# A hybrid decoder layer: all mixers ahead of the feed-forward, and gate and up projections of two token blocks as seven products of halves

## The chip, the core and the metric

The kernel runs on one core of a Trainium2 chip. A core has five engines that work side by side, each with its own queue of instructions in a fixed order: TensorE (PE in the profile, its weight loads PEld) multiplies matrices from SBUF into PSUM; VectorE (DVE), ScalarE (ACT) and GpSimd (POOL) do elementwise work; SyncE (SP) issues most transfers between HBM and SBUF. Semaphores order them. The metric is the device time of one execution in microseconds (us), as the median of several runs. A profile is one further execution, taken by the hardware profiler.

## What is computed

One decoder layer over 2048 tokens of width 1024, in float32. The part that the change touches most is the feed-forward; the mixer ahead of it is only reordered.

```python
mod = silu(c) @ w_ada + b_ada
shift1, scale1, gate1, shift2, scale2, gate2 = split(mod, 6)
h = rmsnorm(x, norm1_w) * (1 + scale1) + shift1
x = x + gate1 * hybrid_mixer(h, ...)        # in-projection, attention and SSD scan, out-projection
h = rmsnorm(x, norm2_w) * (1 + scale2) + shift2
g, u = split(h @ w_gate_up, 2)              # 1024 -> 2 x 2816
x = x + gate2 * ((silu(g) * u) @ w_down)    # 2816 -> 1024
return rmsnorm(x, final_norm_w)
```

The mixer projects h to queries, keys, values, a gate z, a convolution input x/B/C and step sizes; it runs sliding-window attention (window 128, 8 heads, learned sinks) and a chunked state-space scan (SSD, chunks of 128 tokens, with a state carried from chunk to chunk) side by side, concatenates both and projects back.

## The kernel before

Activations are kept transposed: channels on the 128 partitions, tokens along the free dimension. The 2048 tokens are NB = 4 blocks of T = 512. Every operand of a matmul is split into a high part in the reduced float32r format and a low part, the remainder (ScalarE copies to the high part, VectorE or GpSimd subtracts), and a product is three matmuls, high x high, high x low and low x high (`mm3`, L194). A full tile product is 128 x 128 weights by 512 tokens.

*Stages of a block.* `norm1` (L239) squares and sums eight tiles of x, takes the inverse root (`rstd`, `rsqrt`), spreads it over partitions with a matmul (`spread`, L218) and makes eight pairs `hl` (`modulated`, L226). `in_proj` (L250) makes q, keys and values with 256- and 264-column products, then eight x tiles with 512 columns, each with a convolution (L351) and a tanh, then z (L361). `attentions` (L409) goes through four groups of 128 tokens and, in each, four pairs of heads (`softmax`, L462: row maxima L476, exponentials L481, statistics L478 to L486, normalising L489). `ssd` (L512) does a chunk of the scan; L577 writes the state that the next chunk reads, and L592 scales its output. Both write to `spill` in HBM. `out_proj` (L619) reads it back, multiplies by `wo`, adds the residual (L640), stores to `mid` in HBM, and leaves the second norm's factor in `y_of[b]`. `ffn` (L664) then takes the 22 chunks of 128 feed-forward columns in groups of three (twice of two): 16 tile products each for gate and up (2 x 8 x 3 = 48 matmuls a chunk), tanh and two multiplications on the result (L680 to L682), a split (L684, L685), and after a group the down projection into the eight residual tiles (L715). `finish` (L724) applies the final norm and stores.

*Order.* The stages are Python generators whose `yield`s say how one stage's instructions are interleaved with another's. `mixing` (L812) puts attention and scan steps between the steps of the block's own input projection. Blocks 0 and 1 do their input projections first; afterwards `weave` (L731) runs `ffn(b)` with a side stream beside it: what is left of mixer b + 1 and its output projection. The input projection of block b + 2 comes after `ffn(b)`. The program order is a priority: a scheduler that simulates the engines places each instruction in its engine's queue when its inputs and a buffer are there, earlier lines first, so that later work can fill a gap.

*Buffers.* All tiles come from one SBUF pool and one PSUM pool; a tag with n buffers is a ring, and a new tile waits until the old one's last reader is done. Weights go through four `raw` and four `w` buffers (`weight`, L183), every third subtraction on VectorE where `share` is set, else on GpSimd. PSUM has three banks `d` for dense products, one `n` for norms and one each of `am`, `at`, `sm`, `st` for the mixer.

*Modulation.* `ada` (L121) makes one of 48 columns of `mod` by loading two tiles of `w_ada` and taking two dot products on VectorE (L126). The first sixteen are needed at once, the other 32 are made by `rest_of_ada` (L780), beside input projection 1 and the first chunks of `ffn(0)`.

## Time and profile before

| | |
|---|---|
| timed runs | 2442.79 us median of 3 (2442.18 to 2444.24) |
| span of the profiled execution, first to last instruction | 2447.2 us |
| TensorE busy | 2343.6 us, 96% |
| VectorE busy | 1400.1 us, 57% |
| GpSimd busy | 1037.3 us, 42% |
| ScalarE busy | 990.8 us, 40% |
| moved by DMA | 291.46 MB, 119 GB/s on average |
| weight loads of gate and up | 352 of 256 KB |
| mean granted TensorE clock | 0.988 |

How to read the lines of a profile below. A group's row names its line in the kernel, engine, operation, output tile <- input tiles, shape and count; after the first bar the total busy time in us and the mean of one in ns; after the second bar the time for which the engine sat idle just before these instructions, and which instruction ended that wait. A row of stretches gives start and end in us, the length, then for each engine the busy time with the number of instructions, the granted TensorE clock, the busy share of the DMA engines and their rate. In a timeline row the first number is the start, the second the duration. A digit of the slices is the busy share of a fortieth of the span, in tenths. Matmuls are pipelined: their durations overlap, so that the distance of two starts, not the duration, says what one costs. DMA rows give kilobytes and the median us from issue to landing.

### The profile page before, as it was taken

The numbers are of one execution on the slowest core, as the hardware profiler recorded it, in microseconds if no ns is written. First come the engines' busy times: TensorE is split into PE (matmuls) and PEld (weight loads), VectorE is DVE, ScalarE is ACT, GpSimd is POOL, SyncE is SP. The second block draws the span as 40 slices with busy tenths as digits, with TensorE's granted clock in tenths as the row PEclk, the third lists the DMA queues.
The fourth block names the chain that finished last, engine by engine and source line by source line (L and its number), as shares of the span: only waits on it lengthen the run. The fifth ranks groups of instructions, "written<-read, shape, count | busy, mean of one in ns | idle before, by whom it ended". The sixth has DMA issues, their size and how long they took to land.

```text
span 2447.2 us, 34081 instructions
## 1 busy us (share of the span) xinstructions
PE 2343.6 (96%) x11726; PEld 1958.6 (80%) x11726; DVE 1400.1 (57%) x2847; ACT 990.8 (40%) x2053; POOL 1037.3 (42%) x1014
## 2 busy tenths in 40 slices
PE   4899899899999999999999999999999999999997
PEld 4788777788888788988888878888888887888886
DVE  7878987834354577755543557764554346333325
ACT  3455434333444435644333333654433324222322
POOL 4645454333343456333434336433444333333333
PEclk9999999999999999999999999999999999999999
DMA  7323375433334563232344535223234433533332
GB/s 256 99 70 101 116 250 178 144 91 91 85 90 128 180 200 96 76 90 82 105 126 134 156 111 161 82 65 100 82 112 138 140 114 97 159 89 105 94 95 74
DMA packets 179646, 291.46 MB, mean 119 GB/s; under 512 B 18960, under 2 KB 61968, under 8 KB 179472
## 3 DMA queue, kind: packets, MB, share of 16 engines
q1 hardware_dynamic: 178320, 288.22, 39.2%
q8 instruction: 93, 1.52, 0.3%
q10 hardware_dynamic: 1152, 1.05, 0.1%
q14 instruction: 81, 0.66, 0.1%
HBM read 264.03 MB, written 25.17 MB: 118 GB/s over the span
## 4 chain that ended last, share of the span: by engine, by line
PE 76%; DVE 14%; DMA 4%; ACT 2%; issue 2%; POOL 0%; SPq 0%; ACTq 0%; DVEq 0%; POOLq 0%
PE d L195 21%; PE d L197 21%; PE d L196 21%; DVE it L351 3%; DMA f<-in_wada_dram 2%; PE am L195 2%; PE am L197 2%; PE am L196 2%; DVE f L126 1%; PE sm L195 1%; PE sm L197 1%; PE sm L196 1%; PE sm L556 1%; PE at L496 1%; DVE nh L228 1%
## 5 line engine op out<-in xcount | busy, mean ns | idle before, releaser
L191 POOL TENSOR_TENSOR w<-raw,w 128x512 fp32r<-128x512 f32 (+2 forms) x679 | 855.9, 1266 | 1193.7 <-ACT w L188 1166.8
L188 ACT ACTIVATE w<-raw 128x512 fp32r<-128x512 f32 (+2 forms) x796 | 476.8, 605 | 852.7 <-PE d L197 543.8
L195 PE MATMUL d<-hl,w 128*128 128x512 f32 x1664 | 658.3, 397 | 7.8 <-DVE it L296 5.2
L197 PE MATMUL d<-hl,w 128*128 128x512 f32 x1664 | 659.9, 397 | 0.0
L196 PE MATMUL d<-hl,w 128*128 128x512 f32 x1664 | 658.0, 396 | 0.0
L195 PEld LDWEIGHTS d<-hl,w 128*128 128x128 f32 x1664 | 313.5, 188 | 76.0 <-issue 5.4
L196 PEld LDWEIGHTS d<-hl,w 128*128 128x128 f32 x1664 | 314.2, 189 | 71.9 <-DVE hl L231 0.5
L197 PEld LDWEIGHTS d<-hl,w 128*128 128x128 f32 x1664 | 313.2, 188 | 71.0 <-issue 0.5
L195 PE MATMUL d<-act,w 128*128 128x512 f32 (+1 forms) x720 | 281.4, 402 | 7.2 <-DVE x L715 4.9
L196 PE MATMUL d<-act,w 128*128 128x512 f32 (+1 forms) x720 | 281.4, 392 | 4.6 <-DVE act L685 4.6
L715 DVE SCALAR_TENSOR_TENSOR x<-d,mod,x 128x512 f32<-128x512 f32 (+1 forms) x264 | 189.3, 731 | 168.4 <-PE d L197 168.1
L197 PE MATMUL d<-act,w 128*128 128x512 f32 (+1 forms) x720 | 280.7, 391 | 0.0
L682 DVE SCALAR_TENSOR_TENSOR f<-f,d 128x512 f32<-128x512 f32 x88 | 60.5, 687 | 259.1 <-PE d L197 258.8
L681 DVE SCALAR_TENSOR_TENSOR f<-f,d 128x512 f32<-128x512 f32 x88 | 60.5, 687 | 254.2 <-ACT f L680 254.2
L195 PE MATMUL d<-w,hl 128*128 128x256 f32 (+1 forms) x592 | 170.1, 293 | 5.4 <-ACT hl L230 2.9
L196 PE MATMUL d<-w,hl 128*128 128x256 f32 (+1 forms) x592 | 170.3, 290 | 1.6 <-POOL w L191 1.6
L197 PE MATMUL d<-w,hl 128*128 128x256 f32 (+1 forms) x592 | 166.9, 288 | 4.2 <-DVE hl L231 4.2
L195 PEld LDWEIGHTS d<-act,w 128*128 128x128 f32 x720 | 136.0, 190 | 40.9 <-DVE x L715 10.2
L196 PEld LDWEIGHTS d<-act,w 128*128 128x128 f32 x720 | 136.6, 190 | 33.8 <-DVE act L685 6.8
L197 PEld LDWEIGHTS d<-act,w 128*128 128x128 f32 x720 | 136.3, 189 | 30.3
L195 PEld LDWEIGHTS d<-w,hl 128*128 128x128 f32 x592 | 113.7, 194 | 8.9 <-ACT hl L230 4.5
L197 PEld LDWEIGHTS d<-w,hl 128*128 128x128 f32 x592 | 112.7, 192 | 6.1 <-DVE hl L231 5.2
(328 smaller groups left out, 3373.8 us busy)
## 6 DMA issues: line engine op xcount, KB each, us to landing
raw<-in_wgu_dram SPq DMA_DIRECT2D x352, 256.0 KB, 2.7
raw<-in_wd_dram SPq DMA_DIRECT2D x192, 192.0 KB, 2.4
xt<-in_xT_dram SPq DMA_DIRECT2D x80, 256.0 KB, 3.0
raw<-in_wx_dram SPq DMA_DIRECT2D x64, 256.0 KB, 2.7
f<-in_wada_dram SPq DMA_DIRECT2D x64, 256.0 KB, 3.3
raw<-in_wo_dram SPq DMA_DIRECT2D x64, 256.0 KB, 3.0
xbc<-in_wada_dram SPq DMA_DIRECT2D x32, 256.0 KB, 4.7
raw<-in_wq_dram SPq DMA_DIRECT2D x32, 256.0 KB, 2.8
```

The source lines that it names most:

```text
L126: dot = nc.vector.tensor_tensor_reduce(w, w, csil[half], 0.5, (b_ada if first else part)[:, i:i + 1], ALU.mult, ALU.add, (part if first el ...
L188: nc.scalar.activation(hi, raw[:, :n], AF.Copy)
L191: eng.tensor_tensor(lo, raw[:, :n], hi.bitcast(F32), ALU.subtract)
L195: nc.tensor.matmul(out, ahi, bhi, start=first, stop=False)
L196: nc.tensor.matmul(out, ahi, blo, start=False, stop=False)
L197: nc.tensor.matmul(out, alo, bhi, start=False, stop=last)
L228: nc.vector.scalar_tensor_tensor(h, x, scale, bc, ALU.mult, ALU.mult)
L351: nc.vector.scalar_tensor_tensor(cv, cin[:, i:i + T], conv_w[:, c, i:i + 1], cv, ALU.mult, ALU.add)
L496: nc.tensor.transpose(ps[:, (2 * s + r) * P:(2 * s + r + 1) * P], sm[:, r, s, :], ident)
L681: nc.vector.scalar_tensor_tensor(th, th, 1.0, ps[0], ALU.add, ALU.mult)
L682: nc.vector.scalar_tensor_tensor(a, th, 0.5, ps[1], ALU.mult, ALU.mult)
L715: nc.vector.scalar_tensor_tensor(x, ps, gate2[:, c:c + 1], x, ALU.mult, ALU.add)
```

## The change

The order of the layer becomes: for each of the four blocks, input projection with its own mixer between its steps; the rest of the mixer and the next block's input projection; output projection b - 1 at step HEAD = 9 of input projection b. Only after output projection 3 does the feed-forward begin, with SBUF and PSUM pools of its own. A pool that takes over the memory of a closed one waits tile by tile (`reuse_waits="tile"`), not for the whole.

The feed-forward goes twice through two blocks (s = 0: blocks 0 and 1; s = 1: blocks 2 and 3). `operands` reads the eight x 2 residual tiles of `mid` and makes seven operand sets of four split pairs each: three quarters of h (B11, B21, B22) and four sums (T1 to T4). `quad` makes one chunk of gate and up for 1024 tokens. It sees the weights as a 2 x 2 matrix (gate and up by lower and upper half of the 1024 channels) and h as another (halves of the channels by blocks), and takes Winograd's form of Strassen's seven products in place of eight, each of 4 x 3 matmuls. Four sums of weights are made on GpSimd and split; the results are put together on VectorE, ScalarE and GpSimd. The two activation tiles go to HBM. `down` reads them back, splits them, and multiplies by `w_down` in groups of four chunks into 16 residual tiles; each weight tile now serves two blocks.

In the mixer, attention takes its softmax statistics once for eight heads (`scores`, `probabilities`), with the transposed probabilities and values of the token group before them in between; the scaling of the scan's output moves from VectorE to ScalarE, and sums of squares from VectorE to GpSimd. The 32 late columns of `mod` are spread over the input projections of blocks 1 to 3. Keys and values of block 1 come ahead of its x tiles, as in the other blocks. A factor of one half moves from the activation into `gate2`.

```diff
-GROUPS = (3, 3, 3, 3, 3, 3, 2, 2)
+G = 4
-HEAD, AHEAD, RATIO = 11, 20, 1.4
+HEAD = 9
...
-    def square_into(acc, x, first, eng=nc.vector, tag="nsq"):
+    def square_into(acc, x, first, eng=nc.gpsimd, tag="nh", pool=sb):
...
-            nc.vector.tensor_scalar(y[:, gs], y[:, gs], rs[:, g:g + 1], None, ALU.mult)
+            nc.scalar.activation(y[:, gs], y[:, gs], AF.Copy, scale=rs[:, g:g + 1])
...
+    def probabilities(st, sms, slots):
+        mx, nm, den, es = (st[:, i, :] for i in range(4))
+        ns = len(slots)
+        nc.vector.tensor_scalar(nm, mx, -1.0, None, ALU.mult)
+        nc.vector.tensor_tensor(es, sinks, nm, ALU.add)
+        for i in range(8):
+            sm = sms[i // 2][:, i % 2, 0:ns, :]
+            nc.scalar.activation(sm, sm, AF.Exp, bias=nm[:, i:i + 1], accum_out=den[:, i:i + 1])
...
+        def operands(s, up):
+
+            bc = [spread(y_of[2 * s + j], bc=bank8(), pool=up) for j in range(2)]
+            ops = {n: [] for n in ("b11", "b21", "b22", "t1", "t2", "t3", "t4")}
+            for k in range(4):
+                h = {}
+                for i in range(2):
+                    for j in range(2):
+                        d = k + 4 * i
+                        x = tmp(up, "t", 10)
+                        nc.sync.dma_start(x, mid[2 * s + j][d])
+                        nc.vector.scalar_tensor_tensor(x, x, scl2[:, d:d + 1], bc[j], ALU.mult, ALU.mult)
+                        h[i, j] = x
...
+        def product(out, a, b, first):
+            for k in range(4):
+                ks = slice(k * P, (k + 1) * P)
+                ahi, alo = a[0][:, ks], a[1][:, ks]
+                bhi, blo = b[k]
+                nc.tensor.matmul(out, ahi, bhi, start=first and k == 0, stop=False, skip_group_check=True)
+                nc.tensor.matmul(out, ahi, blo, start=False, stop=False, skip_group_check=True)
+                nc.tensor.matmul(out, alo, bhi, start=False, stop=k == 3, skip_group_check=True)
+
+        def quad(s, f, ops, up):
+            a11, a21, a22, a12 = (load_w(wgu[f, u, half]) for u, half in ((0, 0), (1, 0), (1, 1), (0, 1)))
+            w11 = halves(a11, nc.vector)
+            s1, s2, s3, s4 = (tmp(fw, "s", 4) for _ in range(4))
+            nc.gpsimd.tensor_tensor(s1, a21, a22, ALU.add)
+            nc.gpsimd.tensor_tensor(s2, s1, a11, ALU.subtract)
+            ws2 = halves(s2, nc.gpsimd)
+            ws1 = halves(s1, nc.vector)
+            nc.gpsimd.tensor_tensor(s3, a11, a21, ALU.subtract)
+            ws3 = halves(s3, nc.gpsimd)
+            w12 = halves(a12, nc.vector)
+            nc.gpsimd.tensor_tensor(s4, a12, s2, ALU.subtract)
+            ws4 = halves(s4, nc.gpsimd)
+            w22 = halves(a22, nc.vector)
+
+            pa, pb, pc, pd = bank8(), bank8(), bank8(), bank8()
+            u2, u3, c22 = tmp(up, "t", 10), tmp(up, "t", 10), tmp(up, "t", 10)
+            product(pa, w11, ops["b11"], True)
+            nc.scalar.activation(u2, pa, AF.Copy)
+            product(pb, ws2, ops["t2"], True)
+            nc.vector.tensor_tensor(u2, u2, pb, ALU.add)
+            product(pc, ws1, ops["t1"], True)
+            nc.scalar.activation(c22, pc, AF.Copy)
+            product(pd, ws3, ops["t3"], True)
+            nc.vector.tensor_tensor(u3, u2, pd, ALU.add)
+            nc.gpsimd.tensor_tensor(c22, c22, u3, ALU.add)
+            product(pa, w12, ops["b21"], False)
...
+            nc.scalar.activation(g1, pa, AF.Tanh, scale=0.5)
+            nc.vector.scalar_tensor_tensor(g1, g1, 1.0, pa, ALU.add, ALU.mult)
+            product(pc, ws4, ops["b22"], False)
+            nc.vector.tensor_tensor(c12, u2, pc, ALU.add)
+            nc.scalar.activation(g2, c12, AF.Tanh, scale=0.5)
+            nc.vector.scalar_tensor_tensor(g2, g2, 1.0, c12, ALU.add, ALU.mult)
+            nc.gpsimd.tensor_tensor(g2, g2, c22, ALU.mult)
+            nc.sync.dma_start(act_d[s][f, 1], g2)
+            product(pd, w22, ops["t4"], False)
+            nc.vector.tensor_tensor(u2, u2, pd, ALU.add)
+            nc.vector.tensor_tensor(g1, g1, u2, ALU.mult)
+            nc.sync.dma_start(act_d[s][f, 0], g1)
+
+        def down(s, dn):
+            x2 = [[big("x2", 16, pool=dn) for _ in range(2)] for _ in range(KT)]
+            for c in range(KT):
+                for j in range(2):
+                    nc.sync.dma_start(x2[c][j], mid[2 * s + j][c])
+            for g in range(6):
+                n = G if g < 5 else NF - 5 * G
+                act = []
+                for i in range(n):
+                    for j in range(2):
+                        a = big("ar", 4, pool=dn)
+                        nc.sync.dma_start(a, act_d[s][g * G + i, j])
+                        hi, lo = pair("a", 16, pool=dn)
+                        nc.scalar.activation(hi, a, AF.Copy)
+                        lower(lo, a, hi)
+                        act.append((hi, lo))
...
+                if g < 5:
+                    for c in range(KT):
+                        w = halves(load_w(wd4[g, c]), nc.gpsimd if c % 2 else nc.vector)
+                        for j in range(2):
+                            columns(c, j, slice(0, T), w, 0)
...
+    for b in range(NB):
+        if side is not None:
+            drain(side)
+            before = out_proj(b - 1, y_of)
+        gen = in_proj(b, h, own, after_first)
+
+        def every(i, b=b):
+            if b > 0:
+                for _ in range(3 if b == 1 and i < 2 else 1):
+                    next(ada_rest, None)
+            if i == HEAD and b > 0:
+                drain(before)
...
+    drain(side)
+    drain(ada_rest)
+    drain(out_proj(NB - 1, y_of))
+    mixer.close()
```

380 lines of the change are left out of this document (170 added, 210 removed).

## The prediction, made before the changed kernel was run

> **What bounds the kernel now.** I read the page first (shares, slices, chain), then the stretches between stages, then single instructions by form, then the end of the timeline.
>
> ```profile
> span 2447.2 us, 34081 instructions
> PE 2343.6 (96%) x11726; PEld 1958.6 (80%) x11726; DVE 1400.1 (57%) x2847; ACT 990.8 (40%) x2053; POOL 1037.3 (42%) x1014
> ...
> PE   4899899899999999999999999999999999999997
> ...
> DVE  7878987834354577755543557764554346333325
> ...
> PE 76%; DVE 14%; DMA 4%; ACT 2%; issue 2%; POOL 0%; SPq 0%; ACTq 0%; DVEq 0%; POOLq 0%
> ```
>
> TensorE sets the time: it is busy 96% and holds 76% of the chain. The exception is the first eight slices, where VectorE is at 70 to 90% and TensorE has gaps. The stages, cut at instructions of the timeline (first row: the last tanh of block 0's z projection; second: the first tanh of a feed-forward):
>
> ```profile
> L361 ACT ACTIVATE it<-d x8: 362/382/390, 151.8 to 171.5; 128x256 f32<-128x256 f32 x8
> ...
> L680 ACT ACTIVATE f<-d x88: 577/599/602, 432.6 to 2411.2; 128x512 f32<-128x512 f32 x88
> ```
> ```profile
> core 0: us, PE busy (x) PEld busy (x) DVE busy (x) ACT busy (x) POOL busy (x), PEclk, DMA share, GB/s
> 0.00:171.00 171.00, 126.59 (x792) 114.09 (x793) 136.43 (x307) 81.16 (x177) 89.07 (x154) 0.97 0.47 150
> 171.00:433.00 262.00, 236.97 (x1341) 203.22 (x1340) 228.68 (x540) 119.40 (x279) 128.44 (x125) 0.95 0.49 154
> 433.00:900.00 467.00, 458.32 (x2183) 378.30 (x2182) 246.92 (x482) 189.12 (x389) 178.12 (x147) 1.00 0.41 119
> 900.00:1020.00 120.00, 118.23 (x767) 106.09 (x766) 93.21 (x223) 66.34 (x153) 68.43 (x84) 1.00 0.40 122
> ...
> 2430.00:2447.00 17.00, 2.96 (x12) 1.57 (x11) 12.14 (x43) 0.84 (x3) 2.56 (x4) 0.66 0.38 124
> ```
> ```profile
> 2200.00:2250.00 50.00, 50.00 (x217) 40.31 (x216) 15.01 (x21) 14.81 (x27) 18.16 (x17) 1.00 0.32 95
> ```
> ```profile
> 943.39 0.28 PE L195 MATMUL am<-k_ring,qT 128*128 128x256 f32 x1
> 943.51 0.27 PE L196 MATMUL am<-k_ring,qT 128*128 128x256 f32 x1
> ```
>
> From these come my units. A product of 512 columns costs 50/217 = 0.2304 us of TensorE, one of 256 columns 0.12 us (943.39 to 943.51). A feed-forward block is 22 x 48 + 22 x 24 = 1584 products = 365.0 us, four are 1459.8 us. The stretch 433 to 2430 (1997 us) holds those and two input projections, three mixers and three output projections, so these cost 1997 - 1460 = 537 us where the feed-forward lies over them. An input projection is 192 x 0.2304 + 480 x 0.12 = 101.8 us, an output projection 192 x 0.2304 = 44.2; that leaves 537 - 203.6 - 132.6 = 201, or 67 us for a mixer. In 171 to 433 there is no feed-forward: input projection 1, output projection 0, about two thirds of mixer 0 and a little of mixer 1 (101.8 + 44.2 + 45 + 10 = 201 us by these prices) took 262 us, 1.30 times as long, with VectorE busy 228.7/262 = 87%.
>
> **The products.** For each of the 22 column chunks and a pair of blocks, seven products of 4 x 3 matmuls (84) replace 2 x 48 = 96. Over 2 x 22 that is 528 matmuls fewer: -121.7 us (the counts are in the loop bounds, so that the change might not do this is no rival). The down projection keeps its 2 x 1056. New TensorE time of the feed-forward: 2 x 1848 x 0.2304 = 851.6 us, and 486.6 us.
>
> The Trainium skill, page "TensorE: Matmul & The Clock Gate", section "Back-to-back issue gap", gives about 131 ns for a sustained 512-column product; by that the saving would be estimated at 528 x 0.131 = 69 us only. The trace here has 230 ns, and I take it.
>
> **Do the other engines keep up with 84 matmuls (19.4 us)?**
>
> ```profile
> L191 POOL TENSOR_TENSOR w<-raw,w 128x512 fp32r<-128x512 f32 x459 | 617.5, 1349 | 874.5 <-ACT w L188 848.3 <-DVE f L682 15.1 <-DVE x L715 7.1
> L188 ACT ACTIVATE w<-raw 128x512 fp32r<-128x512 f32 x576 | 360.6, 630 | 578.2 <-PE d L197 381.8 <-POOL w L191 96.5 <-issue 40.8
> ...
> L715 DVE SCALAR_TENSOR_TENSOR x<-d,mod,x 128x512 f32<-128x512 f32 x248 | 181.8, 747 | 165.3 <-PE d L197 165.0
> L191 DVE TENSOR_TENSOR w<-raw,w 128x512 fp32r<-128x512 f32 x117 | 81.2, 694 | 33.5 <-ACT w L188 33.2
> L205 DVE TENSOR_TENSOR nacc<-nacc,nsq 128x512 f32<-128x512 f32 x73 | 65.5, 898 | 22.5 <-ACT nsq L204 21.2
> L231 DVE SCALAR_TENSOR_TENSOR hl<-nh,mod,hl 128x512 fp32r<-128x512 f32 x64 | 59.5, 938 | 1.7 <-ACT hl L230 1.3
> L126 DVE CUSTOM_DVE_ANT_0 f<-f,act,part 128x512 f32<-128x512 f32 x32 | 34.5, 1080 | 8.3 <-DMA f<-in_wada_dram 8.2
> L228 DVE SCALAR_TENSOR_TENSOR nh<-xt,scl,n 128x512 f32<-128x512 f32 x32 | 22.8, 738 | 2.9 <-PE n L223 2.8
> L485 DVE TENSOR_TENSOR ast<-ast 128x2 f32<-128x2 f32 x64 | 18.5, 289 | 21.5 <-ACT ast L484 21.3
> L478 DVE TENSOR_SCALAR ast<-ast 128x2 f32<-128x2 f32 x64 | 18.4, 287 | 0.4
> L592 DVE TENSOR_SCALAR sy<-sy,rs 128x256 f32<-128x256 f32 x32 | 16.0, 538 | 0.4
> L126 DVE CUSTOM_DVE_ANT_0 f<-f,act,vec 128x512 f32<-128x512 f32 x32 | 29.4, 921 | 11.6 <-DMA f<-in_wada_dram 11.6
> ```
>
> Per quad GpSimd has nine operations (four sums of weights, three low halves, two on results): 9 x 1.35 = 12.1 us. ScalarE has 7 splits and 4 evictions, 11 x 0.63 = 6.9. VectorE has 4 low halves and 7 on results, 11 x 0.75 = 8.3. All fit under 19.4, and nine weight pairs hold eight products (22 us) of lead, so I cost them at nothing; without that cover they are the second rival. In the down projection the re-read activations add 8 splits and 8 low halves to 44 us of products, well under it too. Half as many gate and up loads, 88 activation writes and 88 re-reads about cancel on SP's queue.
>
> **The mixers without cover.** They must now run against their own projections. What changes on VectorE: the squares' sums go to GpSimd (per block 14 of the row at 0.90: 11 us, 12 with rounding), the y scaling to ScalarE (16.0/4 = 4), the softmax statistics run once for eight heads instead of four times for two (three quarters of 18.5 + 18.4 in two rows alone, 7 per block), and the later modulation dots (34.5 + 29.4 = 63.9 us, some nine tenths of them in 171 to 433) are spread, 21 per block. The stretch 171 to 433 would have had 228.7 - 58 + 21 - 22 = 170 us of VectorE. At the 87% it reached, that is 195 us, against 201 us of TensorE: TensorE binds again, by little. With two engines so near each other I add 6%; the ends are 0% (as under the feed-forward) and 30% (as in 171 to 433). From 171 to the end of the last input projection: 3 x 101.8 + 3 x 44.2 + 3 x 67 = 639, x 1.06 = 677 us. The first 171 us stay.
>
> Then the rest of mixer 3 lies bare, with nothing behind it but its own 45 us of TensorE. In the first stage its recurrence advanced like this:
>
> ```profile
> L577 DVE TENSOR_TENSOR state<-state,sm x3: 674/675/675, 224.2 to 298.6; 128x512 f32<-128x512 f32 x3
> ```
>
> Two steps in 74.4 us, 37 each, while sharing VectorE with a projection; four such steps would be 149 us. Ends 45 and 149; alone I take half of the latter, 75 us. Output projection 3 follows: spill, reload and split before its first matmul, then 44.2 us bare.
>
> ```profile
> out_dram<-x SPq DMA_DIRECT2D x24, 256.0 KB, 3.9
> mix<-ao SPq DMA_DIRECT2D x16, 256.0 KB, 2.5
> ...
> xt<-mid SPq DMA_DIRECT2D x8, 256.0 KB, 2.8
> ```
>
> 2.5 out, about 2.8 in, 0.63 and 0.9 to split and start-up: 8 us, so 52.
>
> **The seams.** The operands of a group cost VectorE, for each of four k, 4 x 0.74 + 3 x 0.94 + 4 x 0.9 = 9.4 us, 37 in all, and the first product needs every k. The first group is blocks 0 and 1, whose norms are long known; what waits is memory still held by output projection 3, about a third: 12 us (ends 0 and 37). Up to down, twice: the activations come through four buffers, eight tiles to a group, so two rounds of load 2.8, high 0.63, low 1.35, partly before the last product: 8 us each (ends 2 and 20, the latter if the 16 residual loads go first on SP). Down to the second group:
>
> ```profile
> 2430.18 0.28 PE L197 MATMUL d<-act,w 128*128 128x256 f32 x1
> ...
> 2440.95 3.22 DVE L728 SCALAR_TENSOR_TENSOR x<-x,vec,at 128x256 f32<-128x256 f32 x8 [1.32 <-PE at L223]
> ```
>
> From the last matmul to the first scaled output is 10.8 us; the residual tiles stand where new operand tiles go, so then output store 3.9, load 2.8 and up to 37 us of operands, of which some 18 can be done with tiles freed by the half that finished first: 36 us (ends 18 and 55). The end stays at 17.
>
> Small edits at nothing: keys and values of block 1 ahead of x, one buffer for the inverse root (VectorE is in order anyway, so little to lose), the new pools, HEAD from 11 to 9. Their cover is the other block's products; if it is gone they are in the 6%.
>
> Sum: 171 + 677 + 75 + 52 + 12 + 851.6 + 486.6 + 2 x 8 + 36 + 17 = 2394 us, against the profiled 2447.2. The three timed runs have a median of 2442.79, 4.4 lower, with no work outside the span to be added; I take 4.4 off: 2390 us. In other words 122 us won, about 68 lost again.
>
> By the same page's section "HAM oscillation — how this bites in real kernels", an idle gap over about 3.4 us drops TensorE to half clock for a window; over five seams I estimate 5 x 1.7 = 8 us more. The last stretch above, at a granted 0.66, agrees that idle TensorE loses clock.
>
> **Rivals.**
> - *VectorE keeps the mixers.* If the operations moved away only filled its waits (L485 was idle 21.5 us for ScalarE), the stretch needs 228.7 - 58 + 21 = 192, /0.87 = 220 us, 1.10 times; and busier GpSimd slows VectorE's two-input operations (0.69 for a quiet low half, 0.94 for L231), so 1.18: 639 x 1.18 = 754 (+77), mixer 3's rest 95 (+20), the first seam 36 (+24). 2394 + 121 - 4 = 2511 us, slower. It decides once the factor passes 1.15 (+54). For it: 1.30 measured; against it: much of that stretch was the dots and their loads.
> - *GpSimd's chain stalls each quad.* If the next quad's sums queue behind this quad's last multiplication: product six ends at 16.6, then 0.69 + 0.60 + 0.69 + 1.35 = 19.9; two sums 22.6, split 24.6; TensorE wants it at 19.4 + 2.8 = 22.1. 2.5 x 42 = 105 us: 2495, slower. Against it: GpSimd waits 848 us for ScalarE in the row above, that is, weights are prepared as buffers come free, ahead of the products.
> - *The cover is not missed.* 0% instead of 6% (-38), mixer 3's rest 60 (-15), seams 12 + 36 halved (-24): 2313 us. For it: 900 to 1020, an input projection with mixer work, has VectorE at 78% and TensorE at 98.5%.
>
> **How the numbers follow.** Forecast 0.57 (its own range 2350 to 2440), VectorE 0.18, GpSimd 0.13, cover not missed 0.12. About 0.2% (5 us) is what a measurement here can tell from none. Faster: 0.57 x 0.9 + 0.12 = 0.63; same 0.04; slower 0.33. The range 2320 to 2495 leaves out the half of the third rival below it and most of the first above.
>
> **What would show it.** The products: TensorE near 50 of 50 us in the quads, 217 matmuls per 50 us; below 205, GpSimd's chain. The mixers: output projection 3 should end near 975 us of the span; after 1030, VectorE. VectorE's share before that should be under 80%. The seams: gaps in TensorE of about 8 and 36 us; a 36 us gap also ahead of the first group would make it the first rival's. The forecast fails if mixers and seams together give back more than 122 us.

## The result, and the profile after

| | before | changed |
|---|---|---|
| timed runs, median of 4 | 2442.48 us (2439.54 to 2444.24) | 2615.73 us (2613.50 to 2617.65) |
| changed / before, 95% interval | | 1.0703, 1.0687 to 1.0718 |
| span of the profiled execution | 2447.2 us | 2614.0 us |
| mean granted TensorE clock | 0.988 | 0.933 |

The change made the kernel 7% slower where 2% faster was forecast. The page of the changed kernel, in the lines that answer to those of before:

```profile
span 2614.0 us, 32592 instructions
...
PE 2288.0 (88%) x11198; PEld 1911.6 (73%) x11198; DVE 1447.6 (55%) x2706; ACT 970.0 (37%) x1969; POOL 1285.4 (49%) x1141
...
PE   4888879897988797859999997999599999979995
...
DVE  8778844986387527295444444444764434434435
...
PEclk9999879898989898969999998999699999989997
...
PE 66%; DVE 21%; DMA 4%; issue 3%; POOL 3%; ACT 3%; SPq 0%; POOLq 0%; DVEq 0%; ACTq 0%
```

TensorE has 528 matmuls fewer and 55.6 us less to do, but is busy for 88% of a longer span instead of 96%. Its gaps fill the first seventeen slices, where VectorE jumps between 2 and 9 from slice to slice, and then stand alone at four places, the seams, and at the end. The next view is that of stretches (start and end, length, busy time of PE, PEld, DVE, ACT and POOL with instruction counts, granted clock, DMA share, rate): three periods of the mixing stage, each from one block's last z projection to the next's, the rest of mixer 3, the operands ahead of each group, and 50 us of quads.

```profile
175.00:457.00 282.00, 236.74 (x1366) 203.58 (x1364) 190.46 (x457) 138.83 (x334) 136.41 (x133) 0.90 0.45 138
457.00:721.00 264.00, 225.26 (x1332) 195.99 (x1332) 186.16 (x426) 129.11 (x303) 134.89 (x135) 0.92 0.41 126
721.00:980.00 259.00, 227.74 (x1332) 197.65 (x1332) 158.10 (x376) 125.13 (x296) 121.49 (x126) 0.92 0.32 95
980.00:1056.00 76.00, 52.04 (x293) 43.31 (x291) 54.58 (x141) 35.50 (x106) 20.80 (x20) 0.86 0.11 29
...
1105.00:1163.00 58.00, 27.61 (x67) 16.07 (x68) 52.67 (x68) 22.11 (x38) 43.69 (x28) 0.66 0.42 140
...
1400.00:1450.00 50.00, 50.00 (x222) 41.40 (x222) 19.14 (x27) 16.54 (x28) 31.95 (x25) 1.00 0.28 85
...
1842.00:1905.00 63.00, 29.89 (x72) 17.88 (x71) 45.04 (x76) 18.32 (x31) 27.14 (x19) 0.62 0.32 108
```

Two things are to be seen. The quads run as they should: TensorE 50 of 50 us, 222 matmuls where the kernel before did 217 (experiment 7 is about that difference). And in the three mixing periods neither engine is full: TensorE 84 to 88%, VectorE 68, 71 and 61%, with TensorE's clock at 0.90 to 0.92. Two timeline rows give the ends of that stage, the tanh of block 3's z projection and the residual of output projection 3 (count, durations, first and last time):

```profile
L361 ACT ACTIVATE it<-d x8: 364/380/384, 963.1 to 980.7; 128x256 f32<-128x256 f32 x8
...
L653 DVE SCALAR_TENSOR_TENSOR xt<-sm,mod,xt x4: 744/751/752, 1070.8 to 1104.7; 128x512 f32<-128x512 f32 x4
```

The account against the forecast's sum of 2394 us, from the starts and ends of the same instructions; for the matmuls of quads and down projection the start-to-start time of 226.7 ns is taken, and what a stretch took beyond it is a seam:

| term | forecast | measured | difference |
|---|---|---|---|
| to the end of the last input projection | 171 + 677 = 848 | 980.7 | +133 |
| rest of mixer 3, output projection 3 | 75 + 52 = 127 | 124.7 | -2 |
| first seam, until quads run at full rate | 12 | 45.9 | +34 |
| quads, 3696 matmuls | 851.6 | 837.9 | -14 |
| up to down, twice | 16 | 19.1 + 19.7 | +23 |
| down, 2112 matmuls | 486.6 | 478.8 | -8 |
| gaps inside the down projections | none | 13.8 + 26.3 | +40 |
| down to the second group | 36 | 51.4 | +15 |
| tail | 17 | 16 | -1 |
| sum | 2394 | 2614 | +220 |

The 528 matmuls saved are 119.7 us at 226.7 ns each. The 14 and 8 us below the forecast in the quads and the down projections have another source: a matmul there takes 226.7 ns instead of the 230.4 that the forecast took (231.7 on average in the feed-forward of the kernel before). Against the forecast, 133 us went in the mixing stage, 3 of them ahead of block 1 (block 0's z ends at 174 us), and 112 us in seams.

### The profile page after: what moved, and what is told of

It reads as the page before. It is cut to its first block, busy times and chain, and to the rows that moved or that the text cites. A ratio compares the mean times of both kernels' runs of the same rounds, so it can differ in the third digit from the quotient of the medians.

```text
span 2614.0 us, 32592 instructions
## 1 busy us (share of the span) xinstructions
PE 2288.0 (88%) x11198; PEld 1911.6 (73%) x11198; DVE 1447.6 (55%) x2706; ACT 970.0 (37%) x1969; POOL 1285.4 (49%) x1141
## 4 chain that ended last, share of the span: by engine, by line
PE 66%; DVE 21%; DMA 4%; issue 3%; POOL 3%; ACT 3%; SPq 0%; POOLq 0%; DVEq 0%; ACTq 0%
PE q L732 10%; PE q L733 10%; PE q L731 10%; PE q L198 6%; PE q L199 6%; PE q L200 6%; DVE it L353 3%; PE d L198 2%; PE d L199 2%; PE d L200 2%; PE am L198 2%; DVE aw L128 2%; PE am L200 2%; PE am L199 2%; POOL acc L208 1%
## 5 line engine op out<-in xcount | busy, mean ns | idle before, releaser
L731 PE MATMUL q<-b,w 128*128 128x512 f32 x1232 | 484.6, 396 | 31.9 <-ACT b L710 27.1
L733 PE MATMUL q<-b,w 128*128 128x512 f32 x1232 | 484.9, 394 | 5.6 <-DVE w L680 5.6
L732 PE MATMUL q<-b,w 128*128 128x512 f32 x1232 | 485.4, 394 | 3.4 <-DVE b L705 2.0
L194 POOL TENSOR_TENSOR w<-raw,w 128x512 fp32r<-128x512 f32 (+1 forms) x220 | 299.8, 1367 | 275.8 <-ACT w L191 274.0
L198 PE MATMUL q<-a,w 128*128 128x512 f32 (+1 forms) x720 | 280.3, 396 | 38.0 <-ACT a L789 38.0
L731 PEld LDWEIGHTS q<-b,w 128*128 128x128 f32 x1232 | 234.7, 191 | 87.9 <-ACT b L710 31.3
L199 PE MATMUL q<-a,w 128*128 128x512 f32 (+1 forms) x720 | 279.3, 388 | 0.0
L200 PE MATMUL q<-a,w 128*128 128x512 f32 (+1 forms) x720 | 278.9, 387 | 0.0
L732 PEld LDWEIGHTS q<-b,w 128*128 128x128 f32 x1232 | 234.7, 190 | 56.9 <-DVE b L705 4.8
L733 PEld LDWEIGHTS q<-b,w 128*128 128x128 f32 x1232 | 234.7, 190 | 54.9 <-DVE w L680 6.5
L800 DVE SCALAR_TENSOR_TENSOR x<-q,mod,x 128x512 f32<-128x512 f32 (+1 forms) x200 | 143.8, 728 | 234.6 <-PE q L200 234.2
L679 ACT ACTIVATE w<-raw 128x512 fp32r<-128x512 f32 x220 | 137.9, 628 | 347.1 <-PE q L200 261.2
L680 POOL TENSOR_TENSOR w<-s,w 128x512 fp32r<-128x512 f32 x132 | 191.5, 1451 | 141.9 <-ACT w L679 141.8
L680 DVE TENSOR_TENSOR w<-raw,w 128x512 fp32r<-128x512 f32 x176 | 154.1, 876 | 135.4 <-ACT w L679 135.2
L191 ACT ACTIVATE w<-raw 128x512 fp32r<-128x512 f32 (+1 forms) x220 | 137.2, 629 | 166.2 <-PE d L200 53.7
L198 PEld LDWEIGHTS q<-a,w 128*128 128x128 f32 x720 | 138.9, 193 | 68.1 <-ACT a L789 39.6
L199 PEld LDWEIGHTS q<-a,w 128*128 128x128 f32 x720 | 137.7, 191 | 28.6 <-issue 1.0
```

Source lines behind the costliest of these rows:

```text
L191: nc.scalar.activation(hi, raw[:, :n], AF.Copy)
L194: eng.tensor_tensor(lo, raw[:, :n], hi.bitcast(F32), ALU.subtract)
L198: nc.tensor.matmul(out, ahi, bhi, start=first, stop=False)
L199: nc.tensor.matmul(out, ahi, blo, start=False, stop=False)
L200: nc.tensor.matmul(out, alo, bhi, start=False, stop=last)
L679: nc.scalar.activation(hi, x, AF.Copy)
```

## The experiments

Where no number of runs is given, a time is that of one run. Seventeen runs of the kernel before, on one chip, lie between 2440.8 and 2452.4 us, and its time beside these runs moved from 2445 to 2451 us, so that a difference of a few us between two kernels says nothing unless a stage of the trace shows it. Up to experiment 5 a cut of code shows the edit to the changed kernel, from experiment 6 on mostly that to the kernel of the run before it.

Theory 1, from the trace: with the feed-forward gone, the output projection of block b - 1 and the mixer of block b exclude each other, because both take the PSUM banks `am` and `sm`, one buffer each. Look at block 2, in the view of stretches:

```profile
603.00:643.00 40.00, 22.88 (x115) 17.00 (x113) 28.13 (x63) 19.62 (x53) 9.46 (x11) 0.79 0.39 119
643.00:683.00 40.00, 39.73 (x173) 31.96 (x174) 6.32 (x14) 20.03 (x46) 24.23 (x19) 1.00 0.51 158
```

and at what stands at the border of the two: attention's last scores in `am`, the row maximum of VectorE that reads them, and TensorE's next matmul into `am`, the output projection's, released by that maximum (`ast L486`):

```profile
641.09 0.39 PE L198 MATMUL am<-k_ring,qT 128*128 128x256 f32 x1 [0.46 <-ACT ao L523]
...
642.64 0.47 DVE L486 CUSTOM_DVE_ANT_0 sm<-am,amask,row 128x256 f32<-128x256 f32 x1
...
643.27 0.47 PE L198 MATMUL am<-qz,w 128*128 128x512 f32 x1 [1.21 <-DVE ast L486]
```

For 40 us attention has the banks, but for 24 matmuls, and TensorE is busy for 22.9 of them; then output projection 1 has them, 168 matmuls in one piece, and VectorE is busy for 6 of 40 us, since scores and scan wait in their turn. Theory 2, the forecast's own first rival, is that VectorE's amount of work sets the period. Later runs add the seams.

### 1. Banks of its own for the output projection

```diff
-            ps = bank(("am", "sm")[c % 2], 1)
+            ps = dense()
```

> The output projection takes its banks from the dense ring of three in place of the mixer's two. Theory 1 (the output projection and the mixer of the next block exclude each other through the banks am and sm): the 40 us stretches of out_proj with an idle VectorE fall away in three blocks; output projection 3 ends near 1000 us of the span in place of 1104, time about 2515 us. Theory 2 (the amount of VectorE's work in a block sets the period of 260 us): no more than 15 us less, since VectorE has as much to do; 2600 to 2620 us.

Measured: 2536.11 us, 79.6 less than the changed kernel. First a stretch of this kernel, then two of its timeline rows:

```profile
597.00:640.00 43.00, 43.00 (x213) 35.80 (x212) 14.73 (x29) 25.90 (x58) 27.87 (x22) 1.00 0.61 189
```
```profile
L361 ACT ACTIVATE it<-d x8: 365/381/386, 889.5 to 906.5; 128x256 f32<-128x256 f32 x8
...
L653 DVE SCALAR_TENSOR_TENSOR xt<-d,mod,xt x8: 749/751/753, 990.8 to 1025.1; 128x512 f32<-128x512 f32 x8
```

The wait of 40 us is gone: TensorE is full, and the last input projection ends at 906.5 instead of 980.7. All 80 us come from ahead of output projection 3's end; the seams are as they were (45.7, 19.4, 50.9 us). Theory 1 holds, for 74 of the 133 us. The edit also gives the output projection a ring of three banks instead of two, but that is not what it lacked: once it had its two banks, in the second row for block 2, TensorE was busy for 39.7 of 40 us. The expected end at 1000 us was 25 us too early; why is not shown (VectorE is still busy for only 14.7 of 43 us in the stretch above).

### 2. The place of the output projection

```diff
-HEAD = 9
+HEAD = 2
```

> HEAD 2 in place of 9: output projection b - 1 stands ahead of the attention of block b in program order, so that the banks am and sm go to it first. Theory 1: the mixer of block b is not cut in two any more; some 20 us less a block, output projection 3 ends near 1045, time about 2555 us. Theory 2: within 15 us of 2616. If the scan of block b - 1 is what the output projection waits for, attention now stands behind it too, and the time goes up by some 10 us a block.

Measured with the old banks: 2593.08 us, 22.7 less, between the two theories; output projection 3 ended at 1085. The order of claims on the banks matters, but standing first in it gains less than a third of what banks of their own gain. With the dense banks, HEAD 3 and HEAD 12 were tried (the latter on the kernel of experiment 6), by the same one-line edit:

> The output projection on the dense banks, and HEAD 3 in place of 9. With its own banks it no longer excludes the mixer, so its place should matter little: within 15 us of 2536. If TensorE's order of work still decides (the x tiles come later behind it, and with them the scan): 15 to 40 us more.

Measured: 2576.96 us, 41 more than with HEAD 9. The forecast of "little" fell, and the second expectation was met within 1 us. Its reason, that the x tiles now come behind the output projection and the scan that needs them starts later, was not tested by itself; block 3's z ended at 942 us instead of 906.

> As the kernel without the pool boundary, with HEAD 12 in place of 9, so that the output projection stands behind the x tiles. HEAD 3 cost 41 us. If the order of x tiles ahead of the output projection is what counts (they feed the scan): 5 to 20 us less than HEAD 9, read at the end of output projection 3 (1025 with HEAD 9). If at 9 nearly all x tiles are ahead already: within 5 us. If the output projection now falls into the time in which z and the rest of the mixer would be covered: up to 15 us more.

Measured: 2505.89 us against 2504.29 with HEAD 9. The input projection of block 3 ended 53 us earlier, at 855, and output projection 3 at 1042 instead of 1048: the order only moves time between the projection and the rest of the mixer, and at this place it has nothing more to give.

### 3. VectorE's load

These two kernels leave the 32 late modulation columns out and use a constant in their place.

```diff
             with tc.issue_after(after_load.ins), tc.issue_after(in_proj.last.ins):
-                ada(i, "aw", 2)
+            if i == 16:
+                nc.gpsimd.memset(mod[:, 16:48], 0.5)
```

> Leaves out the 32 late columns of the modulation (a constant stands in their place), so 64 loads of 256 KB and 64 dot products on VectorE, some 64 us of it, all in the mixing stage. Theory 2 (VectorE's load): some 50 to 64 us less, output projection 3 ends near 1045, time about 2557 us. Theory 1 (banks): under 20 us less, 2596 us or more.

Measured: 2570.51 us, 45.2 less, between the two expectations. On the dense banks:

> Leaves out the 32 late columns of the modulation, with the output projection on the dense banks. The banks took 80 us off the changed kernel, the dots alone 45 us. If the two are separate costs (each of the 64 dots 0.7 us on the mixers' chain): 2536 - 45 = 2491 us, output projection 3 ends near 980. If the dots cost only where the mixers were held up by the banks: 2520 us or more. If they cost more once VectorE is what is left: 2480 us or less.

Measured: 2512.25 us, 23.9 less than with the dots (block 3's z at 880 instead of 906), again between the expectations. So half of what the dots cost was cost only while the banks held the mixers up, and 24 us are left once they do not. These runs leave out the 64 loads with the 64 dots, so they do not tell the two apart. Banks and dots together take away 101 of the 133 us; the other 32 are not taken apart here (the sums of squares on GpSimd and the scaling on ScalarE, for two, were not undone).

The mixer was not only reordered: its softmax is another. This was undone as well, on the dense banks (the attention of before put in for the new one):

```diff
-                sms.append(scores(st, qhi, qlo, slots, j))
...
-            probabilities(st, sms, slots)
-            held = values_of(sms, slots, t)
...
+                sm = softmax(st, qhi, qlo, slots, j)
+                if late is not None:
+                    late()
```

> The output projection on the dense banks, and the softmax of before (statistics for two heads at a time, the transposed probabilities of a pair one pair late). If the statistics for eight heads at once relieve VectorE and so the mixers: 3 x 7 to 3 x 10 us more than 2536, about 2560 us. If their long run of exponentials and normalisations on ScalarE (7 us a token group, during which no scores and no values run) is what stretches the mixers: 20 to 50 us less, about 2500 us.

Measured: 2535.31 against 2536.11 us. Neither expectation: the softmax edit makes no difference that these two runs can tell.

### 4. Eight products in place of seven

```diff
-            s1, s2, s3, s4 = (tmp(fw, "s", 4) for _ in range(4))
...
+            for j in range(2):
+                pg, pu = bank8(), bank8()
+                lo, hi = ops["b1%d" % (j + 1)], ops["b2%d" % (j + 1)]
+                product(pg, w11, lo, True)
+                product(pg, w12, hi, False)
...
+                product(pu, w21, lo, True)
+                product(pu, w22, hi, False)
```

> Gate and up projections by eight products in place of seven, with everything else of the changed order; without the sums of weights and of operands. If the seven products save what their matmuls cost (528 x 0.2252 us): 119 us more in the two quad stretches, less up to 2 x 10 us that the lighter operands save ahead of each group; about 2720 us. If the sums around the products cost TensorE time in the quads: less than 60 us more.

Measured: 2684.43 us, 68.7 more than seven. A stretch of its quads:

```profile
1130.00:1180.00 50.00, 49.81 (x220) 41.26 (x221) 19.18 (x30) 11.27 (x18) 5.23 (x4) 1.00 0.30 93
```

Both kernels do 220 to 222 matmuls in 50 us there, so that 528 more are 119 us. What is missing to 119 stands in the seams: ahead of the first quads 20.3 us instead of 45.9, between the groups 28.9 instead of 51.4, 48 together. The seven products save what their matmuls cost, and the operand sets that they need (28 pairs instead of 16, and the sums) give 48 us of it back, in the two places where nothing covers them.

### 5. The seams: memory, queue order, or work

The down projection's start in the changed kernel, on SyncE's queue, where a row spans from the first to the last issue:

```profile
1572.72 0.33 SPq L774 DMA_DIRECT2D act<-t  x1
1573.14 9.31 SPq L780 DMA_DIRECT2D x<-mid  x16
1582.81 15.73 SPq L787 DMA_DIRECT2D ar<-act  x13
```

The sixteen residual tiles, needed only at the end of a column, go ahead of the activations, needed at once, and both wait until the last quad has gone: they stand behind the last store of a quad's result on this queue, and by the code the new pool stands on the quads' memory. And in the last group of the down projection, TensorE's rows of the norm of one half:

```profile
1823.21 1.87 PE L213 MATMUL q<-ones,acc 128*128 128x2 f32 x8 [2.98 <-POOL acc L208]
...
1828.41 2.08 PE L226 MATMUL q<-nh,ones 128*128 128x512 f32 x2 [3.34 <-DVE nh L224]
...
1830.71 0.63 PE L199 MATMUL q<-a,w 128*128 128x512 f32 x1
1831.14 0.63 PE L200 MATMUL q<-a,w 128*128 128x512 f32 x1
```

The next half's columns are independent of both, but stand behind them in TensorE's queue: 10 us without a column, three times in the kernel. Behind the gap matmuls start 0.43 us apart (the last two rows) instead of 0.227, for the first six or so.

```diff
-            for c in range(KT):
-                for j in range(2):
-                    nc.sync.dma_start(x2[c][j], mid[2 * s + j][c])
...
-                        a = big("ar", 4, pool=dn)
+                        a = tmp(fw, "s", 4)
...
+                if g == 0:
+                    for c in range(KT):
+                        for j in range(2):
+                            nc.sync.dma_start(x2[c][j], mid[2 * s + j][c])
...
+                    for j, ts in todo:
+                        for c in range(KT):
+                            columns(c, j, ts, ws[c // 2], c % 2 * n * P, accs[j])
+                        if late is not None:
+                            norm(*late)
+                        late = (j, ts)
```

> The output projection on the dense banks, and four edits to the seams: the first activations are re-read ahead of the residual tiles, through buffers of the feed-forward's own pool; the two operand rings are laid out so that the first sets stand on memory that comes free early; the mixer's tiles that output projection 3 uses stand under the weights of the feed-forward and not under its operands; and the last norm of one half is put behind the next half's columns. If memory and queue order make the seams (theory): first seam 49 to about 20 us, up to down 20 to about 6 us twice, down to the second group 27 + 28 to about 25, the three norm gaps of 10 us to about 3 each; in all some 100 us less than the 2536 us of the kernel with the dense banks, about 2435 us. If VectorE and GpSimd make the operands too slowly in any case (50 us for the 44 + 16 operations, whenever they start), both operand seams stay above 35 us and the time is above 2480 us.

Measured: 2487.37 us, 48.7 less than with the dense banks alone. Up to down fell from 19.4 and 20.0 to 1.6 us each; the gaps inside the down projections from 13.7 and 26.4 to 2.7 and 11.8, of which the tail took 6 back. Both operand seams stayed (45.8 and 54.8), and the time is above 2480 us, as the second expectation had it: making the operands is too slow in any case. To see why, look at the operations between output projection 3 and full rate in the changed kernel, as groups on VectorE and on GpSimd (busy us and mean ns after the first bar):

```profile
L705 DVE SCALAR_TENSOR_TENSOR b<-t,mod,b 128x512 fp32r<-128x512 f32 x12 | 12.5, 1064 | 0.0
L699 DVE SCALAR_TENSOR_TENSOR t<-t,scl,q 128x512 f32<-128x512 f32 x16 | 11.6, 738 | 1.8 <-DMA t<-mid 1.4 <-PE q L226 0.4
L715 DVE TENSOR_TENSOR t<-t 128x512 f32<-128x512 f32 x4 | 6.3, 1569 | 0.0
```
```profile
L711 POOL TENSOR_TENSOR b<-t,b 128x512 fp32r<-128x512 f32 x14 | 23.1, 1664 | 6.4 <-ACT b L710 6.4
```

VectorE is at work for 52.7 of 58 us there and waits for little. Its operation with one input from PSUM (L699) takes the usual 738 ns; those with two inputs from SBUF take 1064 and 1569 on average, beside a GpSimd that is busy for 43.7 us. One by one, six of the twelve of L705 take 737 to 752 ns and the others 851 to 1768. The Trainium skill, page "SBUF — State Buffer", section "🔬 SBUF: two separate sides", says that VectorE with two SBUF inputs and GpSimd hold one pair of ports in turn, each for a whole instruction; the durations agree with it.

### 6. Starting the operands early

Five of the seven operand sets and the temporaries move into a pool that opens ahead of output projection 3; the down projection uses the sets' own buffers, without a pool of its own, so that the second group's loads stand ahead of the first one's last stores.

```diff
-                hi, lo = pair("b", 28, pool=up)
+                hi, lo = pair(name, 4, pool=SET[name])
...
-                        hi, lo = pair("a", 16, pool=dn)
+                        name = (("b11", "t2"), ("t1", "t3"))[g % 2][j]
+                        hi, lo = pair(name, 4, pool=SET[name])
...
+    early.close()
+    with tc.tile_pool(name="up", bufs=1, reuse_waits="tile") as up:
...
+        drain(out_proj(NB - 1, y_of))
+        mixer.close()
```

> Output projection on the dense banks, last norms behind the next half's columns, and buffers without a pool boundary in the feed-forward: five of the seven operand sets and the temporaries lie in a pool that opens before output projection 3, and the down projection keeps its activations and residual tiles in the operand sets' own buffers, so that the loads of a group's residual tiles no longer stand behind the last stores of the stage before them. If the operand seams come from when the operands may start (theory): 46 us ahead of the first group falls to about 15, 55 us ahead of the second to about 20; some 65 us less than the 2487 us of the kernel with the seam edits, about 2422 us. If VectorE and GpSimd need their 50 us where they are (they are slower while TensorE's other work needs them too): less than 25 us less, 2460 us or more.

Measured: 2504.29 us, 17 more than in experiment 5. The first seam fell to 19.6 us, but output projection 3 ended at 1048 instead of 1029, with VectorE busy for 44.0 and GpSimd for 39.6 of the 48 us ahead of its end; the seam between the groups stayed at 55.3. Two side effects blur the comparison. Every matmul of the feed-forward became slower, 232.0 to 232.7 ns on average instead of 226.8, some 32 us in all (experiment 7), so that without this the edit would by this estimate have won about 15 us. And for the first group the spread norm is now copied to SBUF, while the second group still reads it from PSUM (`q`):

```profile
L707 DVE SCALAR_TENSOR_TENSOR t<-t,scl,bc x16: 737/868/1800, 984.8 to 1041.1; 128x512 f32<-128x512 f32 x16
L707 DVE SCALAR_TENSOR_TENSOR t<-t,scl,q x16: 732/735/747, 1776.6 to 1808.6; 128x512 f32<-128x512 f32 x16
```

The same operation takes 1182 ns on average with the copy and 737 without it, which makes the first group's work 7 us longer. Even with both taken off, the gain stays below the 25 us of the second expectation: an earlier start alone does not remove the operand seams. Then the eight columns of `gate2` went beside the quads:

```diff
-        for i in (*range(16, 24), *range(32, 40), *range(24, 32), *range(40, 48)):
+        for i in (*range(16, 24), *range(32, 40), *range(24, 32)):
...
+                if s == 0 and 4 <= f < 12:
+                    ada(36 + f, "raw", 8, fw)
```

> As the kernel without the pool boundary, with the last eight columns of the modulation (16 dot products, 15 us of VectorE, which only the down projection needs) made beside the quads of the first group. Leaving all 64 dots out took 45 us from the changed kernel, 0.7 us a dot. If the same rate holds: output projection 3 ends 11 us earlier than in the kernel without the pool boundary, and the time is 11 us less. If the dots cost only where the out_proj banks held the mixer up: under 4 us less.

Measured: 2491.08 us, 13.2 less, 0.8 us a dot: a little more than expected. Without any late dot, experiment 3 had won 23.9 us, so these 16 of the 64 have more than half of that; why is not shown.

### 7. Where the operands lie

The feed-forward's pools start at other bytes: one by the padding below, the other because a tile of 192 bytes leaves the memory ahead of it.

```diff
+OFF = 160
...
+        fw.tile([P, OFF], F32, name="pad", tag="pad", bufs=1)
```

> As the kernel with the last modulation columns made late, with the feed-forward's buffers moved by 192 and 832 bytes, so that weights and activations lie as in the changed kernel (byte 160 of 256 on a partition for both). From the starts of its matmuls a 512-column product takes 226.7 ns in the changed kernel, 231 to 232 in the kernel before and 231 to 233 in the last three kernels, whatever else they do. If the place of the operands sets it: 226.7 ns again, 3696 x 4.9 + 2112 x 6.6 ns = 32 us less, 2459 us. If something else in the order of these kernels does: no change, 2491 us.

Measured: 2454.97 us, 36.1 less than 2491.08. The view of stretches in the quads, first with the buffers as they were in experiment 6 (first kernel), then moved:

```profile
1300.00:1350.00 50.00, 50.00 (x217) 40.37 (x216) 19.65 (x28) 16.68 (x29) 32.28 (x24) 1.00 0.25 83
```
```profile
1300.00:1350.00 50.00, 50.00 (x222) 41.42 (x221) 18.81 (x27) 16.54 (x28) 32.04 (x25) 1.00 0.27 85
```

217 against 222 matmuls at full clock, by a shift of some hundred bytes.

### 8. Doing the operands' work elsewhere

For the second group, scaled tiles, biases and sums are made beside the first group's quads and kept in HBM; between the groups they are only loaded and split. For the first group the low halves of the sums go to VectorE.

```diff
+        def prepare(bc, k):
...
+            nc.vector.tensor_tensor(x, h[0, 1], h[0, 0], ALU.subtract)
+            put("t1", x)
...
-            ops = operands(s, up)
+            ops = prepared() if s else operands(s, up)
```

> As the aligned kernel, and two edits to the operands: for the first group the low halves of the four sums go from GpSimd to VectorE; for the second group scaled tiles, biases and sums (32 of VectorE's operations) are made beside the quads of the first group and kept in HBM, so that between the groups only loading and splitting are left. Starting the operands early had brought next to nothing: full rate of TensorE was reached at about 1080 us with and without it, since VectorE and GpSimd were full while they were made. If this work is the seam (theory): the stretch from the last matmul of the first down projection to full rate falls from some 60 us to about 30, and the one ahead of the first group by 5 to 10; about 2425 us, faster than before. If the wait for residual tiles to be stored and reloaded is: under 10 us less, 2450 us.

Measured: 2449.26 us (10 runs), ratio to the kernel before 1.0017 (1.0007 to 1.0026). The seam between the groups fell from 55 to 40 us, half of what was expected, and only 6 us were won, since the first group's quads took 440.8 us instead of 430.2. The expected 2425 us was missed; the time is that of the second expectation, but not for its reason, as the seam did get shorter. A stretch of the quads:

```profile
1340.00:1360.00 20.00, 16.32 (x73) 13.21 (x71) 18.47 (x20) 8.80 (x17) 11.65 (x9) 0.99 0.64 213
```

VectorE is at 92% there, with the preparation in one go, and TensorE loses 4 us. So the preparation was spread over more quads, and the dots over blocks 1 to 3:

```diff
+                if s == 0 and 10 <= f < 22:
+                    with tc.issue_after(quad.last.ins):
...
+                        next(todo, None)
...
-                for _ in range(3 if b == 1 and i < 2 else 1):
+                if b > 1 or i < 5:
```

> As the kernel with prepared operands, with two edits: the preparation is spread over quads 6 to 21 of the first group, each piece behind the end of a quad, and its two spreading matmuls come two quads behind their diagonals; and the dots of the modulation are spread over blocks 1 to 3 in place of mostly block 1. The first group's quads lost 11 us of TensorE in two places of the prepared kernel (4 us at the spreading matmul, 7 us where VectorE was 92% busy with preparations in one go). If that is their cause: 10 us less, and 0 to 8 us less in the mixers for the dots; 2434 us, below the kernel before by 0.4%. If quads and preparation collide on VectorE in any case: within 4 us of 2449.

Measured: 2443.93 us (12 runs), ratio 0.9994 (0.9982 to 1.0006), where 2434 was expected. The first group's quads are back at 429.2 us, as expected; the dots in block 3 were a mistake, since mixer 3's end moved from 953 to 965 and output projection 3's from 1027 to 1039. The seam is still 41 us, and 33 of them are TensorE ahead of the final norm:

```profile
1734.48 2.07 PE L233 MATMUL q<-nh,ones 128*128 128x512 f32 x2 [14.93 <-DVE nh L231]
...
1756.00 2.07 PE L233 MATMUL q<-nh,ones 128*128 128x512 f32 x2 [17.96 <-DVE nh L231]
```

The last run takes the dots back to their place and moves that norm beside the second group's quads:

```diff
+                    if sq is not None and s == 0:
+                        nc.sync.dma_start(fin[j, c], x)
...
-                        if late is not None:
+                        if late is not None and s == 1:
                             norm(*late)
...
+                if s == 1 and 7 <= f < 15:
...
+                            nc.sync.dma_start(x, fin[j, d])
+                            nc.vector.scalar_tensor_tensor(x, x, fw_[:, d:d + 1], fdg[j], ALU.mult, ALU.mult)
+                            nc.sync.dma_start(outT[j, d], x)
```

> As the kernel with the preparation spread out, without its edit of the dots, and with the final norm of the first group's two blocks taken out from between the groups: the residual results and their sums of squares are kept, and scaled and stored beside the second group's quads 1 to 14. In the last two kernels TensorE stood 15 and 18 us in front of the two spreading matmuls of that norm, 1719 to 1757 us. If that wait is what is left of this seam: 25 to 30 us less, about 2417 us, faster than before by 1%. If the operands of the second group (28 splits on ScalarE, 28 subtractions) take the same time there: under 8 us less, 2436 us or more.

Measured: 2420.05 us (4 runs) against 2447.67 for the kernel before beside it, ratio 0.9884 (0.9867 to 0.9901): 1.2% less than the kernel before, clear of the noise. Its page and the stretch between the groups:

```profile
span 2419.9 us, 32754 instructions
...
PE 2227.7 (92%) x11198; PEld 1885.2 (78%) x11198; DVE 1524.0 (63%) x2724; ACT 973.5 (40%) x1987; POOL 1271.5 (53%) x1123
```
```profile
1712.00:1731.00 19.00, 6.99 (x24) 4.88 (x24) 8.19 (x9) 7.80 (x14) 18.92 (x15) 0.68 0.32 112
```

The seam is 16 us, with GpSimd full in it. That does not yet show that the new order wins. In this kernel a matmul of the feed-forward takes 226.7 ns and in the kernel before 231.7, and 5 ns in each of its 5808 are 29 us, as much as the 28 us between the two kernels. Nobody moved the buffers of the kernel before as experiment 7 did here; whether it would then be as fast stays open.

## Why the prediction was wrong

**The products.** Right: TensorE is full in the quads, 528 matmuls are 119 us (experiment 4), and GpSimd's chain did not stall them; that rival falls. By the section of the Trainium skill that the prediction weighed, "TensorE: Matmul & The Clock Gate", "Back-to-back issue gap", the saving would have been 69 us; the run with eight products shows the trace's price. That experiment 4 measures 68.7 us in the end is a coincidence: it is 119.7 us of matmuls less 48 of seams. What the step left out is that the operands of seven products are 48 us dearer than those of eight at the seams. And 22 us that the forecast did not have came from where the changed kernel's buffers happen to lie: luck.

**The mixers without cover.** This is the step that failed, at "TensorE binds again, by little. With two engines so near each other I add 6%". The stretch from 171 us to the end of the last input projection took 810 us, a factor of 810/639 = 1.27 instead of 1.06. I added up two engines' work and took the larger, as if both could always run. They could not: output projection and mixer took turns on two PSUM banks. Without that the factor was (906 - 171)/639 = 1.15, and without the late dots 1.11. In the kernel before, by its code, the same banks are shared in the same way, but there the feed-forward runs on other banks meanwhile. The cover that the change took away hid a conflict between stages, not only latency.

**Rest of mixer 3, output projection 3.** 124.7 us for 127. The 52 for the output projection was worked out; the 75 for the mixer was a point taken halfway to the upper end of a range of 45 to 149, and that it was hit is in part luck.

**The seams.** All too small: 12 for 46, 8 for 19, 36 for 51 us, and the 10 us gaps of the norms were not in the sum. For the first and third the size was off because the operands were priced at 0.74 to 0.94 us per operation from rows with a quieter GpSimd, and because the first was taken as one third of that work, waiting for memory; experiment 6 shows that early memory moves the work more than it shortens the seam. For the second, the end of 20 us that the prediction named, residual tiles first on SyncE, is what happened, and I had taken the middle.

**The rivals.** "VectorE keeps the mixers" gave 2511 us and the right sign, but its mechanism is a part only: VectorE was busy for (190.46 + 186.16 + 158.10)/805 = 66% of the three periods, below the 80% that the prediction had set as VectorE's mark, and the runs give 24 to 45 us to the dots and 74 to 80 to the banks. The marker "after 1030, VectorE" was therefore badly chosen: output projection 3 ended at 1105 and it was mostly something else.

**The clock.** The prediction, in its sentence on the Trainium skill, gave 8 us to cold TensorE at five seams, outside its sum, and nothing in the mixers. The section of the Trainium skill that it names counts half of a throttled 1.67 us as lost, so that by it the estimate should have been 4 us. In the trace the matmuls behind the 10 us gap at 1820 us lose about 2 us. And the rows show a granted clock of 0.62 to 0.66 in the operand seams and 0.90 to 0.92 over whole mixing periods: there gap follows gap, and the matmuls between them are slow. How much of the 133 us that is was not measured by itself.

## What to carry to other kernels

When a change takes away the work that covered a stage, list what the stage's parts share (banks, buffers, one place in a queue) before adding up engines: a shared resource with one buffer makes two parts run one after the other, and no engine's share of busy time shows it. Price the preparation of a cheaper algorithm where nothing runs beside it, with the durations of a loaded neighbour engine. And move such work under a stage with slack, in small pieces; starting it earlier beside something that needs the same engines mostly moves the loss.

## What the runs showed of the hardware

A 512-column float32r matmul with its weight load takes 226.7 ns from start to start, or 231 to 233 on average, depending on where its two operands lie in SBUF. In the feed-forward of the changed kernel the intervals are 226.7 ns (standard deviation 0.7), in that of the kernel before 231.7, in the three kernels from experiment 6 up to the move 231.6 to 232.7. Experiment 7 moved the buffers alone and got the 226.7 back, 36 us. As the kernels are built, weights and activations both start at byte 160 of 256 on a partition in the fast ones, and in experiment 6's first kernel the weights at byte 224 and most activations at 160. Equal places alone do not make it fast: in that kernel two of the seven operand sets lie at 224 like the weights, and take 232.4 ns. Which rule of addresses lies behind it stays open; 160 for both is the place that was seen to be fast.

VectorE with two inputs from SBUF is slowed by a busy GpSimd, with one from PSUM it is not: 1182 against 737 ns for the same operation in one kernel (experiment 6), and 738 ns in the changed kernel's first seam, where GpSimd was busy for 43.7 of 58 us.
